# Dilated attention with scores in 64x32 fp32 tiles, values per four blocks, and a bias table spread by class late in the program

## The chip, the cores and the metric

The kernel runs on one core of a Trainium2 chip, as one launch. The metric is the device time of a run in microseconds (us). The core has a matrix engine (PE, with its weight loads shown apart as PEld), a vector engine (DVE), a scalar engine (ACT), a general engine (POOL), and a queue (SP) from which this kernel issues nearly all of its DMA transfers. Each engine works through its own list of instructions in order and waits by semaphores for the others.

## The reference

One transformer block in fp32: 1024 tokens, width 1024, eight attention heads and eight gated DeltaNet heads of 64 side by side, then a gated feed-forward part. The attention is dilated in three branches that are merged by their log-sum-exp, which is one softmax over keys of different multiplicity:

```
DILATED_BRANCHES = ((128, 1), (512, 4), (2048, 16))
...
    steps = qi + band - kj
    in_window = (steps >= 0) & (steps <= band)
    bias = rel_bias.astype(jnp.float32)[_t5_bucket(jnp.maximum(steps, 0) * dilation)]
    s = jnp.einsum('bhrnqd,bhrnkd->bhrnqk', qb * dh ** -0.5, kw) + bias[None, :, None, None]
...
    w = jax.nn.softmax(jnp.stack(lses), axis=0)
    o = jnp.sum(w[..., None] * jnp.stack(outs), axis=0)
```

A query sees every key at a distance of up to 128, and further back only keys at a distance that is a multiple of 4 (up to 512) or of 16. Keys farther than one block of 128 thus count only if they have the query's position modulo 4, its class. The DeltaNet half takes projections q, k, v through a causal convolution of width 4 and SiLU, solves a unit triangular system in each chunk of 64, and scans over 16 chunks.

## The kernel before

The program has stages one behind another. From the start to about 100 us it normalizes and projects. delta(0) and then delta(1) treat four DeltaNet heads each: preparation, convolution of v (`delta_v`), a triangular inverse (`delta_inverse`), and a scan over chunks (`delta_scan`). Then `attend` does the attention, for four pairs of heads (hp) and eight query blocks of 128 (qb), 32 units in all; the output projection follows, and from about 720 us the feed-forward part, which the change leaves alone.

PE is kept at work by fill. `fill[0]` is a generator of projection matmuls: in delta(1) these are the gate projection `g_z`, the attention projections `g_a` (queries and keys) and `g_va` (values), and later the output projection `wo`. `turn(name)` asks the table FILL how many us of fill go ahead of a step, `ahead` takes them, and in `attend` a budget FRONT is spread over the first units. With these settings the library that builds the program sets the final order of each engine's list.

In delta(1) three chains meet. The first is v: a load `xp_v` per pair of heads (`fetch`, `_.pj`), the convolution taps on ACT and DVE (tile `vd`, lines L550 and L552), SiLU on ACT (L556), transposes on PE (`trv`, L874), and a scaling on DVE (`vb`, L877). It runs for two pairs. The second is the inverse on DVE: tile `nt` is loaded from `lt_d` (L852), scaled (L887), and 31 steps of two instructions follow (`tm` L898, `tt` L902). The third leads from the inverse to the scan: `tt` is written out as `tn_d`, read back as `tn` (L905, L907), turned on DVE (`U`, L935), and used by PE for `lv` (L930).

The attention of a unit (hp, qb): scores `S` of a head against all keys up to the query's block. They are made in fp32r (a faster fp32 mode of PE) with K split in a high and a low part (`KS`, `KL`) and Q in a tile `QS` of 128 rows that carries both parts of Q, so that two matmuls of up to 512 columns make one stretch of scores (L1327, L1328). `att_load` makes these tiles for every head on ACT, DVE and POOL. DVE adds the bias and takes the running minimum of the negated scores (L1331), ACT takes the exponential (L1336), POOL scales by the reciprocal of the sum (L1338). One unit later (AT=1) PE transposes the result block by block (`tr`, L1351), which ACT and DVE copy to `et`; three units later (AV=3), for two units at a time, PE multiplies by the values (`y`, L1372), a head in each half of the columns of the array.

The bias is a table `R_d` of 1152 numbers for each head (negative scores, with a huge number where a key is not seen). When the values of the first pairs are stored (`va`, L1102), eight broadcast transfers spread a row of it over 128 rows as `Rb_d` (L1121, 576 KB each); in the profile they are issued at 69 to 79 us. `att_load` reads a skewed view of it as `ng` (512 KB for a head).

## Time and profile before

| what | value |
|---|---|
| runs | 1385.23, 1391.03, 1392.99 us, median 1391.03 |
| profiled execution | 1385.31 us, its span 1383.3 us |
| PE, DVE, ACT, POOL busy | 1336.5, 875.4, 659.7, 268.4 us |
| chain that ended last | PE 71%, DVE 14%, DMA 5%, ACT 4% |
| attention with its fill on PE | 451.6 to 654 us |

A number is one execution's. Busy time of PE is nearly the whole span, but a busy PE is not a PE at its peak: matmuls are pipelined, and an instruction's duration holds its latency. What one costs is seen from the distance of one start to the next. Where an engine idles, the row of the instruction behind the gap shows in square brackets how long it waited and for whom.

### The profile page before, as it was taken

Reading aid. Unit: us, or ns where it says so; the run is one execution under the profiler, and the core shown is the slowest. Engines: PE = TensorE matmul, PEld = TensorE weight load, DVE = VectorE, ACT = ScalarE, POOL = GpSimd, SP = SyncE. Lnnn points to the kernel's source line nnn. Section 1 sums busy time; section 2 is a strip of 40 time slices with the busy share of each in tenths; the row PEclk is TensorE's granted clock in tenths of the full one; section 3 lists DMA queues with packets and bytes.
Section 4 is the critical chain, followed back from the end, with each engine's and each line's share of the span. In section 5 each row is a group of like instructions: output and inputs, shape, how many; then the busy total and the mean of one; then the engine's idle time right before and its main releaser. Section 6 shows DMA issues by size and latency. Waiting matters only on the chain.

```text
span 1383.3 us, 24383 instructions
## 1 busy us (share of the span) xinstructions
PE 1336.5 (97%) x8984; PEld 1105.9 (80%) x8984; DVE 875.4 (63%) x1678; ACT 659.7 (48%) x1285; POOL 268.4 (19%) x250
## 2 busy tenths in 40 slices
PE   8998999999999999999999999999999999999998
PEld 5777887888889877687877788888888888888876
DVE  3688583657847242766248978666675776474497
ACT  4497514347233454775168633333333333454455
POOL 2345303324213434542261000000000000000000
PEclk9999899999999999999999999999999999999999
DMA  8665574475362546531675346445453665765585
GB/s 313 228 191 171 163 212 159 138 221 164 120 175 82 170 139 178 150 100 66 211 242 168 113 154 209 142 160 175 151 177 123 218 215 183 251 226 193 191 272 192
DMA packets 169871, 245.64 MB, mean 178 GB/s; under 512 B 32566, under 2 KB 73831, under 8 KB 169752
## 3 DMA queue, kind: packets, MB, share of 16 engines
q1 hardware_dynamic: 169752, 244.08, 54.7%
q8 instruction: 71, 1.16, 0.3%
q14 instruction: 48, 0.39, 0.1%
HBM read 181.27 MB, written 67.48 MB: 180 GB/s over the span
## 4 chain that ended last, share of the span: by engine, by line
PE 71%; DVE 14%; DMA 5%; ACT 4%; issue 3%; POOL 2%; SPq 0%; POOLq 0%; DVEq 0%; ACTq 0%
PE wua L1621 9%; PE wga L1621 8%; PE X L1821 6%; PE wgc L1621 4%; PE wuc L1621 4%; PE g_a L589 4%; PE wo L589 3%; PE Z L1821 3%; PE Y L1821 2%; PE wub L1621 2%; PE wgb L1621 2%; PE y L1372 2%; PE g_va L615 2%; DVE tm L898 2%; PE f L250 2%
## 5 line engine op out<-in xcount | busy, mean ns | idle before, releaser
L1611 DVE TENSOR_TENSOR wl_db<-wr_db,wh_db 128x512 fp32r<-128x512 f32 x77 | 53.0, 691 | 67.2 <-ACT wh_db L1610 67.0
L1610 ACT CAST wh_db<-wr_db 128x512 fp32r<-128x512 f32 x77 | 47.4, 620 | 86.3 <-PE X L1821 37.8
L1331 DVE CUSTOM_DVE_ANT_0 X<-S,ng 128x512 f32<-128x512 f32 (+3 forms) x64 | 36.6, 587 | 60.9 <-PE S L1328 53.7
L1338 POOL TENSOR_SCALAR X<-X,sc 128x128 f32<-128x128 f32 (+7 forms) x64 | 48.6, 762 | 90.5 <-DVE sc L1337 77.5
L1821 PE MATMUL X<-wl_db,wh_da 128*128 128x512 f32 x160 | 62.4, 390 | 0.3 <-DVE wl_db L1611 0.3
L1821 PE MATMUL X<-wh_db,wl_da 128*128 128x512 f32 x160 | 62.3, 389 | 0.0
L1821 PE MATMUL X<-wh_db,wh_da 128*128 128x512 f32 x160 | 62.2, 389 | 0.0
L1336 ACT ACTIVATE X<-X,sc 128x128 f32<-128x128 f32 (+7 forms) x64 | 49.4, 773 | 26.7 <-DVE sc L1331 25.1
L1611 DVE TENSOR_TENSOR wl_da<-wr_da,wh_da 128x512 fp32r<-128x512 f32 x77 | 52.9, 687 | 3.5 <-ACT wh_da L1610 3.5
L1610 ACT CAST wh_da<-wr_da 128x512 fp32r<-128x512 f32 x77 | 47.4, 616 | 14.0 <-DMA wr_da<-ao_d 7.1
L589 PE MATMUL wo<-yh,wh_wo 128*128 128x512 f32 x128 | 52.0, 406 | 0.0
L589 PE MATMUL g_a<-hh,wh_a 128*128 128x512 f32 x128 | 51.4, 402 | 0.0
L589 PE MATMUL wo<-yh,wl_wo 128*128 128x512 f32 x128 | 51.1, 399 | 0.0
L589 PE MATMUL wo<-yl,wh_wo 128*128 128x512 f32 x128 | 50.6, 395 | 0.5 <-DVE yl L1439 0.5
L589 PE MATMUL g_a<-hl,wh_a 128*128 128x512 f32 x128 | 50.6, 396 | 0.0
L589 PE MATMUL g_a<-hh,wl_a 128*128 128x512 f32 x128 | 50.4, 394 | 0.0
L1351 PE MATMUL tr<-ident,X 128*128 128x128 f32 x288 | 44.1, 277 | 4.3 <-ACT et L1356 1.6
L1610 ACT CAST wh_wg_s<-wg_s 128x512 fp32r<-128x512 f32 x33 | 20.6, 623 | 56.1 <-PE wuc L1621 23.8
L1351 PEld LDWEIGHTS tr<-ident,X 128*128 128x128 f32 x288 | 32.6, 140 | 15.3 <-POOL X L1338 6.8
L1610 ACT CAST wh_wg<-wr_wg 128x512 fp32r<-128x512 f32 x31 | 19.3, 621 | 46.2 <-PE wua L1621 18.9
L1610 ACT CAST wh_wu_s<-wu_s 128x512 fp32r<-128x512 f32 x33 | 20.4, 621 | 43.6 <-PE wga L1621 17.2
L230 POOL TENSOR_TENSOR wl_wo<-wr_wo,wh_wo 128x512 fp32r<-128x512 f32 x24 | 31.8, 1326 | 48.5 <-ACT wh_wo L229 44.3
(554 smaller groups left out, 4341.9 us busy)
## 6 DMA issues: line engine op xcount, KB each, us to landing
wm<-in_wada SPq DMA_DIRECT2D x44, 512.0 KB, 6.4
wr_da<-ao_d SPq DMA_DIRECT2D x77, 256.0 KB, 2.9
wr_wu<-in_wu SPq DMA_DIRECT2D x50, 256.0 KB, 2.8
wr_wg<-in_wg SPq DMA_DIRECT2D x48, 256.0 KB, 2.9
ao_d<-a SPq DMA_DIRECT2D x44, 256.0 KB, 2.5
wr_wd<-in_wdn SPq DMA_DIRECT2D x44, 256.0 KB, 3.0
wr_db<-wt_d SPq DMA_DIRECT2D x44, 256.0 KB, 2.7
ao_d<-as SPq DMA_DIRECT2D x33, 256.0 KB, 2.0
```

The lines of the kernel that those rows point to most:

```text
L230: (eng or nc.gpsimd).tensor_tensor(out=lo[:, :n], in0=raw[:, :n], in1=hi[:, :n].bitcast(F32), op=ALU.subtract)
L250: nc.tensor.matmul(first[bank], a[:, w0], b[k][:, cs], start=(k == 0 and n_ == 0), stop=(k == KT - 1 and n_ == 2))
L589: last[0] = nc.tensor.matmul(ps, a[:, w0], b[k0 + k4][:, cs], start=(i == 0), stop=(i == n - 1))
L615: last[0] = nc.tensor.matmul(ps[:, :n], a[k][:, ts_], b[:, w0], start=(i == 0), stop=(i == 23))
L1331: nc.vector.tensor_tensor_reduce(out=X[:, c0:c1], in0=ps[:, 0 : c1 - c0], in1=ng[:, u + c0 : u + c1], scale=1.0, scalar=(3e38 if m is None ...
L1336: nc.scalar.activation(X[:, 0:nk], X[:, 0:nk], AF.Exp, scale=-1.0, bias=m, accum_out=sc[:, 2:3])
L1338: nc.gpsimd.tensor_scalar(out=X[:, 0:nk], in0=X[:, 0:nk], scalar1=sc[:, 3:4], scalar2=0.0, op0=ALU.mult, op1=ALU.add)
L1351: nc.tensor.transpose(ps[:, (kb - c0) * P : (kb - c0 + 1) * P], X[:, kb * P : kb * P + P], ident)
L1610: nc.scalar.copy(hi, src)
L1611: (eng or nc.vector).tensor_tensor(out=lo, in0=src, in1=hi.bitcast(F32), op=ALU.subtract)
L1621: nc.tensor.matmul(ps, a[:, w0], b, start=(first and k == 0 and n_ == 0), stop=(k == 3 and n_ == 2), skip_group_check=True,)
L1821: nc.tensor.matmul(bank[b], a[:, ts_], w, start=(first and n_ == 0), stop=(last and n_ == 2), skip_group_check=True,)
```

## The change

It rewrites the attention and the way of its bias table.

- Table: it holds 1120 numbers sorted by class (448, 448, 224) in place of 1152. It is first copied into `R4_d` (four rows a head, one for each class, four transfers of 8x2x256 and one of 32x1x224), then spread to `Rb_d` by eight transfers of 4x32x736 (377 KB each, in rows of 2944 bytes). They are issued behind the stores of the first values (`table`, called in `va_end`), in delta(1).
- Storing: `spill` writes queries and keys sorted by class in each block (position 4j+r goes to 32r+j), with the factor -0.125 on queries, on ACT. The values are stored sorted likewise.
- Loading: q and k come once for a pair of heads, without the split tiles: four casts and products on ACT, DVE and POOL for each head are gone. The bias tile `bt` (480 columns a head) takes four loads a pair, the values one load and eight small ones (`vf`, the far keys' values).
- Scores: plain fp32, in tiles of 64 rows by 32 columns of the array: two heads (row halves) times four classes (column quarters). A block has eight matmuls against its 256 near keys and, from block 2 on, eight against the 32n far keys of its own class, chained by `issue_after`. A head's row of scores is at most 480 wide and one DVE instruction treats it.
- Transposes: 1, 2, 3, 3, 3, 3, 4, 4 for a head's blocks 0 to 7 (184 in all, 288 before), two units behind the scores (AT=2).
- Values: once for four blocks, 120 matmuls of 64x128, 64 of 64x2x32 and 32 of 64x4x32 (288 of 64x128 before).
- Fill: entries of FILL for the old steps go, and BACK spreads the output projection evenly over the units behind the first 14, 12 matmuls a unit.

Cut to its core:

```diff
-XB, ETB, AT, AV = 5, 6, 1, 3
+XB, ETB, AT, AV = 8, 4, 2, 3
+BACK = 16 * 4 * 0.64
...
+        for h in {3: (0, 1), 4: (2, 3), 5: (4, 5), 6: (6,), 7: (7,)}.get(tb, ()):
+            nc.sync.dma_start(
+                bass.AP(
+                    tensor=Rb_d.tensor, offset=Rb_d[h, 0:1, :].offset + 96,
+                    ap=[[32 * 768 - 32, 4], [768, 32], [1, 736]],
+                ),
+                bass.AP(tensor=R4_d.tensor, offset=R4_d[h, 0:1, :].offset, ap=[[736, 4], [0, 32], [1, 736]]),
+            )
...
-                nc.sync.dma_start(Rb_d[tb], R_d[tb : tb + 1, :].to_broadcast([P, 1152]))
+                with tc.issue_after(stored[0].ins):
+                    table(tb)
...
-                nc.tensor.matmul(ps[:, 0 : c1 - c0], QS[:, qs], KS[:, c0:c1], start=True, stop=False)
-                nc.tensor.matmul(ps[:, 0 : c1 - c0], QS[:, qs], KL[:, c0:c1], start=False, stop=True)
+            for near in range(0 if f else 1, 2):
+                for r in range(4):
+                    for e in (1, 0):
+                        rows, qs = slice(64 * e, 64 * e + 64), slice(32 * r, 32 * r + 32)
+                        if near:
+                            out, src = pss[e][qs, f:w], k[rows, b0 * P : n * P + P]
+                        else:
+                            out = pss[e][qs, 0:f].rearrange("p (m j) -> p m j", j=32)
+                            src = by_class(k[rows])[:, 0:n, r]
+                        with tc.issue_after(mm.ins) if mm else ExitStack():
+                            mm = nc.tensor.matmul(out, by_class(q[rows])[:, n, r], src, start=True, stop=True)
...
+            if i >= first:
+                ahead(BACK / (len(units) + AV - first))
...
-            if i >= AV and units[i - AV][1] % 2:
+            if i >= AV and units[i - AV][1] % 4 == 3:
```

Instructions also change places outside the attention. The first place is DVE in delta(1), around the convolution of v for the second pair (`vd_4040` before, `vd_4046` now) and the inverse, which begins with `nt`. DVE before:

```order
L552 SCALAR_TENSOR_TENSOR vd_4040<-xp_v_4041,cw,vd_4040 128x1023
L552 SCALAR_TENSOR_TENSOR vd_4040<-xp_v_4041,cw,vd_4040 128x1022
L552 SCALAR_TENSOR_TENSOR vd_4040<-xp_v_4041,cw,vd_4040 128x1021
L887 TENSOR_TENSOR nt_3827<-nt_3827,bpr_3829 128x1024
L877 TENSOR_TENSOR vb_4048<-trv_0_4049,beta 128x512
L877 TENSOR_TENSOR vb_4048<-trv_1_4192,beta 128x512
L898 TENSOR_TENSOR tm_0_4202<-nt_3827,tt_4199 128x31
L902 TENSOR_TENSOR tt_4199<-tt_4199,tm_0_4202 128x31
L898 TENSOR_TENSOR tm_1_4205<-nt_3827,tt_4199 128x60
```

The taps of the second pair stood ahead of the inverse. DVE now, first at the head of the inverse:

```order
L862 TENSOR_TENSOR vb_3842<-trv_0_3843,beta 128x512
L862 TENSOR_TENSOR vb_3842<-trv_1_4040,beta 128x512
L872 TENSOR_TENSOR nt_3830<-nt_3830,bpr_3832 128x1024
L883 TENSOR_TENSOR tm_0_4208<-nt_3830,tt_4205 128x31
L887 TENSOR_TENSOR tt_4205<-tt_4205,tm_0_4208 128x31
```

The products of the first pair are followed by `nt` at once. And DVE now at the end of the inverse, 58 rows on:

```order
L883 TENSOR_TENSOR tm_30_4298<-nt_3830,tt_4205 128x31
L887 TENSOR_TENSOR tt_4205<-tt_4205,tm_30_4298 128x31
L537 SCALAR_TENSOR_TENSOR vd_4046<-xp_v_4047,cw,vd_4046 128x1023
L537 SCALAR_TENSOR_TENSOR vd_4046<-xp_v_4047,cw,vd_4046 128x1022
L537 SCALAR_TENSOR_TENSOR vd_4046<-xp_v_4047,cw,vd_4046 128x1021
L862 TENSOR_TENSOR vb_4054<-trv_0_4055,beta 128x512
L862 TENSOR_TENSOR vb_4054<-trv_1_4198,beta 128x512
L920 STREAM_TRANSPOSE U_0_4635<-tn_4302 32x8x32 x4
```

The three taps and the two products `vb` have moved behind the last step of the inverse, next to `U`.

The same pair's transposes `trv` on PE, which read `vd`, before (row 1500 of PE's list, 229 rows ahead of the first `lv`):

```order
L615 MATMUL g_z_4_4301<-wl_z_0_4056,hh_93 128x256
L615 MATMUL g_z_4_4301<-wh_z_0_4055,hh_94 128x256
L874 MATMUL trv_0_4049<-ident,vd_4040 128x128 x4
L874 MATMUL trv_1_4192<-ident,vd_4040 128x128 x4
L615 MATMUL g_z_4_4301<-wh_z_0_4055,hl_102 128x256
L615 MATMUL g_z_4_4301<-wl_z_0_4056,hh_94 128x256
```

And now (row 1549, 183 rows ahead of `lv`; the rows between are 48 `g_z`, 96 `g_a` and 39 `g_va`):

```order
L600 MATMUL g_z_5_4335<-wh_z_3_4079,hl_108 128x256
L600 MATMUL g_z_5_4335<-wl_z_3_4080,hh_100 128x256
L859 MATMUL trv_0_4055<-ident,vd_4046 128x128 x4
L859 MATMUL trv_1_4198<-ident,vd_4046 128x128 x4
L600 MATMUL g_z_6_4363<-wh_z_0_4061,hh_93 128x256
L600 MATMUL g_z_6_4363<-wh_z_0_4061,hl_101 128x256
```

They moved down by two groups of `g_z`, and still stand ahead of all the rest of the fill.

The second place is SP's queue, before, where both loads `xp_v` go out early (rows 189 and 192 of its list; `nt` is row 211):

```order
L1210 DMA xp_v_3832<-pj_d 128x1024
L1220 DMA cv_d<-cv_3405 128x1024
L1102 DMA va_d<-va_4_3919 128x2x128
L1210 DMA xp_v_4041<-pj_d 128x1024
L1220 DMA cv_d<-cv_3430 128x1024
```

And now, around `nt` (row 211) and the second `xp_v` (row 221):

```order
L1103 DMA Rb_d<-R_d 4x32x736
L837 DMA nt_3830<-lt_d 128x1024
L1160 DMA wm_4_5080<-in_wada 128x2x512
L1160 DMA wm_6_5082<-in_wada 128x2x512
L1103 DMA Rb_d<-R_d 4x32x736
L1117 DMA va_d<-va_4_3923 32x4x256
L1103 DMA Rb_d<-R_d 4x32x736 x2
L1117 DMA va_d<-va_5_3953 32x4x256
L1103 DMA Rb_d<-R_d 4x32x736 x2
L1117 DMA va_d<-va_6_3983 32x4x256
L1103 DMA Rb_d<-R_d 4x32x736
L1238 DMA xp_v_4047<-pj_d 128x1024
```

One table transfer goes out ahead of `nt`, and seven ahead of the second `xp_v`.

The third place is PE in a late unit of the attention (pair 3, block 6 before, blocks 5 and 3 now). Before, wide matmuls of one head alternate with transposes and fill:

```order
L1327 MATMUL S_6_512_7640<-KS_6968,QS_6967 128x384
L1328 MATMUL S_6_512_7640<-KL_6969,QS_6967 128x384
L1327 MATMUL S_6_0_7649<-KS_6978,QS_6977 128x512
L1328 MATMUL S_6_0_7649<-KL_6979,QS_6977 128x512
L1351 MATMUL tr_5_0_7661<-ident,X_5_7582 128x128 x2
L1327 MATMUL S_6_512_7653<-KS_6978,QS_6977 128x384
L1328 MATMUL S_6_512_7653<-KL_6979,QS_6977 128x384
L1351 MATMUL tr_5_0_7661<-ident,X_5_7582 128x128 x2
L1351 MATMUL tr_5_4_7667<-ident,X_5_7582 128x128 x2
L589 MATMUL wo_1_1_7566<-yh_6713,wh_wo_1_7344 128x512
```

Now the last near scores of one block are followed by the transposes of the block two units back:

```order
L1356 MATMUL S_5_7741<-raw_3_7075,raw_3_7074 32x256
L1356 MATMUL S_5_7740<-raw_3_7075,raw_3_7074 32x256
L1356 MATMUL S_5_7741<-raw_3_7075,raw_3_7074 32x256
L1356 MATMUL S_5_7740<-raw_3_7075,raw_3_7074 32x256
L1356 MATMUL S_5_7741<-raw_3_7075,raw_3_7074 32x256
L1356 MATMUL S_5_7740<-raw_3_7075,raw_3_7074 32x256
L1387 MATMUL tr_3_7771<-ident,X_3_7646 128x128 x3
L1387 MATMUL tr_3_7770<-ident,X_3_7640 128x128 x3
L1356 MATMUL S_6_7783<-raw_3_7075,raw_3_7074 32x192
```

Small matmuls of the two heads take turns, and each unit visits the scores and the transposes once.

More of the change, by code (lines that the diff above doesn't have):

```diff
@@ L179, in build @@
     nc.sync.dma_start(rb[0:32, :], I["rel"])
-    for t, cs in zip(tbl, (slice(0, T), slice(T, T + P))):
+    for t, cs in zip(tbl, (slice(0, 896), slice(896, 1120))):
         nc.sync.dma_start(t, I["tbl"][:, cs])
@@ L1311, in build, with far @@
     loaded = {}
     ybanks = {}
[L1314 to L1330 removed]
+    def far(n):
+        return 32 * n if n > 1 else 0
@@ new lines, in att_score, with att_turn @@
+            X.append(x)
+        return X, mm
+    turned = {}
+    def att_turn(hp, n, X, mm):
+        f = far(n)
+        if n % 4 == 0:
+            for h in (2 * hp, 2 * hp + 1):
+                turned[h] = pa.tile([P, 4, 4, P], F32, name=f"et{h}_{n // 4}", tag="et", bufs=ETB)
+        s0, s1 = (1, 2) if n == 0 else (0, 2 + (n > 1) + (n > 5))
+        cols = {0: f, 1: f + (P if n else 0), 2: 0, 3: P}
+        pss = [tbank(f"tr{2 * hp + e}_{n}") for e in range(2)]
+        with turn(f"et{hp}_{n}"):
+            for e in (1, 0):
+                for i in range(s0, s1):
+                    with tc.issue_after(mm.ins) if mm else ExitStack():
+                        mm = nc.tensor.transpose(
+                            pss[e][:, i * P : i * P + P], X[e][:, cols[i] : cols[i] + P], ident
+                        )
+        for e in (1, 0):
+            (nc.vector.tensor_copy if e else nc.scalar.copy)(
+                turned[2 * hp + e][:, n % 4, s0:s1].rearrange("p b q -> p (b q)"), pss[e][:, s0 * P : s1 * P]
+            )
+        return turned[2 * hp], turned[2 * hp + 1]
@@ L1390, in attend @@
         xs, ets = {}, {}
+        first = EARLY * TB + 3 + AV
         for i in range(len(units) + AV):
@@ L1952, in _bucket_table @@
 def _bucket_table():
-    d = 1023 - np.arange(1152)
+    i = np.arange(64)
+    near = [128 * (1 - q) + 4 * (31 - i) + 3 - t for q in range(2) for t in range(7)]
+    d = np.concatenate([*near, 4 * (255 - np.arange(224))])
     dist_f = np.maximum(d, 1).astype(np.float32)
```

271 lines of the change are left out of this document (132 added, 139 removed).

## The prediction

> **What bounds the kernel now.** I read the page first, then windows over the two stages that the change touches, then the timelines of PE and DVE there, and the chain that ended last.
>
> ```profile
> PE 1336.5 (97%) x8984; PEld 1105.9 (80%) x8984; DVE 875.4 (63%) x1678; ACT 659.7 (48%) x1285; POOL 268.4 (19%) x250
> ...
> GB/s 313 228 191 171 163 212 159 138 221 164 120 175 82 170 139 178 150 100 66 211 242 168 113 154 209 142 160 175 151 177 123 218 215 183 251 226 193 191 272 192
> ...
> PE 71%; DVE 14%; DMA 5%; ACT 4%; issue 3%; POOL 2%; SPq 0%; POOLq 0%; DVEq 0%; ACTq 0%
> ...
> L1331 DVE CUSTOM_DVE_ANT_0 X<-S,ng 128x512 f32<-128x512 f32 (+3 forms) x64 | 36.6, 587 | 60.9 <-PE S L1328 53.7
> ...
> L1336 ACT ACTIVATE X<-X,sc 128x128 f32<-128x128 f32 (+7 forms) x64 | 49.4, 773 | 26.7 <-DVE sc L1331 25.1
> ```
>
> PE is busy nearly all the time and holds 71% of the last chain. So what PE no longer has to do in the attention is time won, and what makes PE stop in delta(1) is time lost. Two windows show both stages (columns: busy time of PE, PEld, DVE, ACT, POOL, then the granted clock, DMA share, GB/s):
>
> ```profile
> 355.00:386.00 31.00, 31.00 (x175) 27.23 (x175) 21.93 (x45) 8.30 (x18) 11.08 (x8) 1.00 0.42 120
> ...
> 451.60:654.00 202.40, 194.65 (x1436) 158.21 (x1436) 100.86 (x316) 119.94 (x267) 85.86 (x88) 1.00 0.45 135
> ```
>
> In the attention DVE and ACT have half of their time free. In the last 31 us of delta(1)'s inverse PE does not rest at all.
>
> **The attention on PE, before.** The fill inside that window is 350 matmuls of 512 columns and 30 of 256 (the same window for these two lines alone):
>
> ```profile
> 451.60:654.00 202.40, 93.69 (x350) 62.95 (x350) 1.00 0.45 135
> ```
> ```profile
> 451.60:654.00 202.40, 3.81 (x30) 3.66 (x30) 1.00 0.45 135
> ```
>
> What one costs is the distance of starts:
>
> ```profile
> 365.67 0.39 PE L589 MATMUL g_a<-hh,wl_a 128*128 128x512 f32 x1
> ...
> 366.35 0.39 PE L589 MATMUL g_a<-hh,wl_a 128*128 128x512 f32 x1
> ```
> ```profile
> 385.97 0.28 PE L615 MATMUL g_va<-wh_va,hl 128*128 128x256 f32 x1
> 386.09 0.28 PE L615 MATMUL g_va<-wl_va,hh 128*128 128x256 f32 x1
> 386.30 1.20 PE L930 MATMUL lv<-tn,dt 32*32 32x32 f32 x64
> ```
> ```profile
> 639.86 0.40 PE L1327 MATMUL S<-KS,QS 128*128 128x512 f32 x1
> 640.10 0.39 PE L1328 MATMUL S<-KL,QS 128*128 128x512 f32 x1
> 640.32 0.40 PE L589 MATMUL wo<-yh,wh_wo 128*128 128x512 f32 x1
> ```
> ```profile
> 647.21 1.06 PE L1351 MATMUL tr<-ident,X 128*128 128x128 f32 x8
> 648.03 0.48 PE L589 MATMUL wo<-yh,wl_wo 128*128 128x512 f32 x1
> ...
> 650.83 3.50 PE L1372 MATMUL y<-et,va 128*64 128x128 f32 x60
> 654.26 0.50 PE L589 MATMUL wo<-yh,wl_wo 128*128 128x512 f32 x1
> 654.60 0.39 PE L589 MATMUL wo<-yh,wh_wo 128*128 128x512 f32 x1
> ```
>
> Fill: three starts in 0.68 us are 0.227 us each, and 0.12 for 256 columns, so 350 x 0.227 + 30 x 0.12 = 83.1 us. The attention itself takes 202.4 - 83.1 = 119.3. Of it, scores: 0.23 us per 512 columns; the loops give 73,728 columns, 33.1 us. Transposes: eight in 0.82, 288 x 0.1025 = 29.5. Values: 60 records in 3.43, 0.057 each; a plain fp32 matmul leaves two records, so 576 x 0.057 = 32.8. These make 95.4; the other 23.9 are changes of shape and waits.
>
> **Part one: the attention after.** Transposes 184 x 0.1025 = 18.9. Values: 304 records of 128 columns and 128 of 64, 304 x 0.057 + 128 x 0.029 = 21.0. Scores have no like in the trace, since no tile of 64 rows by 32 columns runs before. Each direction alone does:
>
> ```profile
> 19.78 0.66 PE L307 MATMUL sums<-sq,onesr 128*32 128x256 f32 x8
> 20.23 1.04 PE L311 MATMUL sums<-xt,wbg 128*32 128x256 f32 x14
> ```
> ```profile
> 319.82 1.05 PE L798 MATMUL kk_q<-qd,kd 64*128 64x128 f32 x14
> 320.71 0.31 PE L798 MATMUL kk_k<-kd 64*128 64x128 f32 x1
> ```
>
> By the transposes a column of a lone fp32 pass takes 0.8 ns. Column quarters: eight passes of 256 columns in 0.45 us, 56 ns for 205, nearly four at once. Row halves: 14 passes of 128 columns in 0.89, 64 ns for 102, with the first one's start-up in it, nearly two at once. The new scores of a pair of heads are 16 passes over 1920 near and 864 far columns, 178,000 columns in all four pairs: 143 us alone, 18 if eight run at once, 40 if only the quarters do. I take 18, since both directions are seen and nothing in the rows speaks against their product; 40 is the bound. The work is then 18 + 18.9 + 21.0 = 58.
>
> Of the 23.9 beside the work I keep 18. The step out of one shape costs 0.34 - 0.23 = 0.11 us (654.26 to 654.60); 32 visits to the scores and 8 to the values, in and out, make 9, transposes some 3, and 6 stay for waits. For waits it speaks that DVE's and ACT's widths fall from 4608 to 2784 columns a head (36.6 and 49.4 us to about 22 and 30), that two units lie between scores and transposes, and that 12 fill matmuls (2.7 us) stand in each late unit. So 76 instead of 119.3: **43 won**. Bounds: 48 with 13 beside the work, 21 with scores at 40. Taking away the casts on ACT, DVE and POOL costs and wins nothing of its own, as these engines wait for PE. Early in the program eight table transfers of 576 KB vanish; I put that at nothing, since DMA has 5% of the last chain in all.
>
> **Part two: delta(1).** The edit puts the table's transfers into SP's queue, and with them the second `xp_v` went back, and the taps of `vd` on DVE behind the whole inverse. PE's `trv`, which needs them, kept its place ahead of 183 fill rows. PE works in order. So it must stand still until the inverse is done. The rows of this chain:
>
> ```profile
> 342.22 3.92 DVE L552 SCALAR_TENSOR_TENSOR vd<-xp_v,cw,vd 128x1023 f32<-128x1023 f32 x3 [0.39 <-ACT vd L550]
> 346.06 1.22 DVE L887 TENSOR_TENSOR nt<-nt,bpr 128x1024 f32<-128x1024 f32 x1
> ...
> 349.25 0.18 DVE L898 TENSOR_TENSOR tm<-nt,tt 128x31 f32<-128x31 f32 x1
> ```
> ```profile
> 378.25 0.19 DVE L902 TENSOR_TENSOR tt<-tt,tm 128x31 f32<-128x31 f32 x1
> 386.27 1.78 DVE L935 STREAM_TRANSPOSE U<-tn 32x256 f32<-32x256 f32 x4 [7.83 <-DMA tn<-tn_d]
> ```
> ```profile
> 346.24 1.07 ACT vd L556
> 347.35 0.67 PE trv L874 x4
> ...
> 378.47 2.92 DMA tn_d<-tt
> 381.40 4.78 DMA tn<-tn_d
> ```
> ```profile
> 342.21 0.34 SPq L852 DMA_DIRECT2D nt<-lt_d  x1
> ```
>
> From the first tap (342.22) to `trv` (347.35) are 5.1 us. The inverse is 1.2 for `nt` and 349.25 to 378.44 for the steps, 30.4 in all. `nt` was there by 346.06. So now: inverse 346.1 to 376.5, `trv` at 381.6, eight transposes 0.9, then the rows up to `lv`: 48 + 39 of 256 columns and 96 of 512, 87 x 0.12 + 96 x 0.227 = 32.2. `lv` starts at 414.7, where it was 386.3: 28.4 later. Nothing hides it: before, the last `g_va` (386.09) ran straight into `lv`, and the fill that PE could do meanwhile stands behind `trv`. On ACT the SiLU waits with two gate activations behind it, on DVE only `vb` and `U`, all within the stop. The round trip of `tn` (7.7 us, 378.47 to 386.18) leaves the path, and `U` is turned ahead: 0.5 won.
>
> Two costs come on top. First, PE's clock after a rest:
>
> ```profile
> 131.30:134.10 2.80, 0.00 (x0) 0.00 (x0) 2.80 (x5) 0.08 (x1) 0.95 (x1) 1.00 0.24 81
> 135.10:145.20 10.10, 10.10 (x76) 10.10 (x76) 7.04 (x12) 10.10 (x33) 2.99 (x2) 0.50 0.65 173
> ```
>
> A rest of some 2.8 us was followed by 10.1 us at 0.50 of the clock, 5 us lost. A rest of over 20 us should do no less: +5, with 0 and 5 as bounds. The Trainium skill ("TensorE: Matmul & The Clock Gate", Part 1) says that about 3.4 us without work halve the clock and about 3.4 us of steady work bring it back; by that the loss would be 1.7 and the sum 3 us lower. The trace shows three times as long a spell.
>
> Second, one table transfer now goes ahead of `nt`: 0 to 3 us, I take 1.5. **Lost: 28.4 + 5 + 1.5 - 0.5 = 34.4.**
>
> **Sum.** Against the profiled execution of 1385.3: 1385.3 - 43 + 34.4 = 1377. The median of the runs is 0.4% above that execution, about as much as a measurement of this kernel can tell from no change (0.5%, 7 us).
>
> **The rivals.**
>
> Row halves take turns: scores at 40, won only 21, 1385.3 - 21 + 34.4 = 1399. It decides from scores of 27 us on (43 - 34.4 = 9 more than 18). For it: no such tile is in the trace. Against: both directions run at once by themselves. Waits in the attention of 20 us more would end there too, but the free time of DVE and ACT speaks against that.
>
> The second `xp_v` comes late, behind seven table transfers:
>
> ```profile
> Rb_d<-R_d SPq DMA_DIRECT2D x8, 576.0 KB, 7.0
> ```
>
> Spread over all DMA engines, 3.0 MB at the 313 GB/s of the page's best slice are 10 us, and `xp_v` lands long before 376. One after another at 7 us each they take 49: `xp_v` at 392, `trv` at 398, 17 more, 1394. Between lies a mechanism with its own price: their outermost dimension is 4, and if only four of the engines carry them, 3.0 MB take four times 9.6, 39 us from 342.5, so `xp_v` at 381, `trv` at 387 or 388 after ACT's first product, 6 more, 1383. The Trainium skill ("DMA: Bandwidth & Descriptors", on why a DMA increments its semaphore by 16, how many engines) has just this: the number is the largest up to 16 that divides the slowest dimension of both sides. No row of before can tell, since its transfers have 128 rows outermost.
>
> The stop does not come, or DVE is done sooner than I read: then only the attention counts, 1342 to 1350. The order of the rows speaks against it.
>
> **How the numbers follow.** The forecast, 1367 to 1386 with its own bounds: 0.50. Row halves in turn, or waits (1390 to 1402): 0.17. The late `xp_v` (1381 to 1395): 0.22. No stop (1342 to 1350): 0.05. A stop as read with more won, 1360 to 1367: 0.06. Faster by over 7 us (below 1378): 0.35 of the forecast's half and the last two, 0.46; slower (above 1392): most of the first rival and some of the second, 0.23; between: 0.31. The range that leaves out no more than 2 in 10 is 1358 to 1401.
>
> **What would show it.** Right: PE idle from about 356 to 381 with the gap put down to `vd` on ACT, a granted clock of 0.5 behind it, `lv` near 418 to 421, scores at some 0.43 us for eight near matmuls, the attention's own share near 76 us. Wrong: no gap ahead of `trv`; scores at twice that; or `xp_v` landing after the inverse.

## The result, and the profile after

The changed kernel takes 1380.03 us (median of 8 runs, 1375.27 to 1382.03), the kernel before 1389.02 us beside it: a ratio of 0.9931, with a 95% interval of 0.9909 to 0.9953, so it is faster by some 0.7%. The prediction was 1377. The profiled execution of the changed kernel took 1375.27 us, the fastest of its eight, 10.0 less than that of before. Inside these 10 us lie two large terms, as forecast: the attention gives 36, the stop in delta(1) takes 28.

The page of the changed kernel (busy time of the engines, PE's busy tenths in 40 slices of 34 us, PE's granted clock in tenths):

```profile
PE 1315.4 (96%) x9440; PEld 1075.4 (78%) x9440; DVE 834.7 (61%) x1604; ACT 618.3 (45%) x1237; POOL 246.2 (18%) x250
...
PE   8998999997599999999999999999999999999998
...
PEclk9999899999799999999999999999999999999999
```

PE is busy 21 us less, and slice 11 (343 to 378 us) is new: PE is busy 5 tenths of it, and its clock falls. Windows over that place show it closer (busy time of PE, PEld, DVE, ACT, POOL, then clock, DMA share, GB/s). Before, PE was busy all 31 us from 355 to 386.

```profile
341.00:355.00 14.00, 5.71 (x29) 5.50 (x28) 7.78 (x21) 0.40 (x2) 0.00 (x0) 0.62 0.59 190
355.00:386.00 31.00, 22.22 (x139) 21.40 (x140) 21.10 (x49) 4.67 (x9) 0.95 (x1) 0.82 0.41 146
```

PE's rows with a wait in brackets, the changed kernel, in delta(1):

```profile
339.74 1.97 PE L859 MATMUL trv<-ident,vd 128*128 128x128 f32 x8 [4.92 <-ACT vd L541]
354.72 0.58 PE L600 MATMUL g_z<-wh_z,hh 128*128 128x256 f32 x1 [8.29 <-ACT zt L621]
362.42 0.39 PE L600 MATMUL g_z<-wh_z,hh 128*128 128x256 f32 x1 [2.50 <-ACT zt L621]
370.15 0.58 PE L600 MATMUL g_z<-wh_z,hh 128*128 128x256 f32 x1 [3.11 <-ACT zt L621]
376.06 0.39 PE L600 MATMUL g_z<-wh_z,hh 128*128 128x256 f32 x1 [1.48 <-ACT zt L621]
380.90 1.10 PE L859 MATMUL trv<-ident,vd 128*128 128x128 f32 x8 [1.70 <-ACT vd L541]
```

The stop is there, but in pieces. PE did not come to `trv` and wait once; it waited four times in `g_z` ahead of it, for the gate activation `zt` on ACT, and only 1.70 us in front of `trv`. ACT itself waited for transfers (ACT, then SP's queue, then the share of busy DMA engines in 40 slices from 340 to 385 us):

```profile
354.28 0.38 ACT L621 ACTIVATE zt<-g_z 128x256 f32<-128x256 f32 x1 [13.27 <-DMA va_d<-va]
...
374.59 1.15 ACT L535 ACTIVATE vd<-xp_v,cw 128x1024 f32<-128x1024 f32 x1 [4.49 <-DMA xp_v<-pj_d]
```
```profile
338.86 0.63 SPq L1103 DMA_DIRECT2D Rb_d<-R_d  x1
339.73 0.34 SPq L837 DMA_DIRECT2D nt<-lt_d  x1
...
359.15 4.21 SPq L1238 DMA_DIRECT2D xp_v<-pj_d  x1
```
```profile
DMA  4969995222522222252226942555258243220640
```

The 2's are the table: a share of two tenths is what 4 of 16 engines make while the other 12 stand idle. The stores of the values behind it in the queue (`va_d`, 14.3 us from issue to landing) keep ACT's buffers. The second `xp_v` left at 359.15 and let ACT begin at 374.59. DVE, in the same order of time:

```profile
347.80 1.23 DVE L872 TENSOR_TENSOR nt<-nt,bpr 128x1024 f32<-128x1024 f32 x1 [5.37 <-DMA va_d<-va]
...
372.27 0.19 DVE L887 TENSOR_TENSOR tt<-tt,tm 128x31 f32<-128x31 f32 x1
375.77 3.92 DVE L537 SCALAR_TENSOR_TENSOR vd<-xp_v,cw,vd 128x1023 f32<-128x1023 f32 x3 [3.31 <-ACT vd L535]
```

In the attention, the window that answers to 451.60:654.00 of before, all lines and then the fill alone; and one stretch of units with blocks 2 to 4:

```profile
484.90:679.20 194.30, 191.61 (x2002) 140.51 (x2002) 75.97 (x255) 83.73 (x226) 66.05 (x89) 1.00 0.53 157
```
```profile
484.90:679.20 194.30, 125.29 (x489) 88.08 (x489) 1.00 0.53 157
```
```profile
605.82 0.78 PE L1356 MATMUL S<-raw,raw 64*32 64x64 f32 x32
606.52 0.44 PE L1387 MATMUL tr<-ident,X 128*128 128x128 f32 x2
609.65 0.83 PE L1356 MATMUL S<-raw,raw 64*32 64x96 f32 x32
610.40 0.66 PE L1387 MATMUL tr<-ident,X 128*128 128x128 f32 x4
...
613.43 0.39 PE L574 MATMUL wo<-yh,wl_wo 128*128 128x512 f32 x1
613.75 0.88 PE L1356 MATMUL S<-raw,raw 64*32 64x128 f32 x32
614.56 0.88 PE L1387 MATMUL tr<-ident,X 128*128 128x128 f32 x6
615.19 0.48 PE L574 MATMUL wo<-yh,wh_wo 128*128 128x512 f32 x1
```

A unit's scores (8 near matmuls and 8 far ones, each of two passes and so two records) take 0.70, 0.75 and 0.81 us up to the transposes: 32 far columns more for each of 16 passes cost 0.055 us. At 0.8 ns a column one after another they would cost 0.41: seven to eight run at once.

### The profile page after: what moved, and what is told of

Same layout as the page of the kernel before. It is cut to its first block, busy times and chain, and to the rows that moved or that the text cites. A ratio compares the mean times of both kernels' runs of the same rounds, so it can differ in the third digit from the quotient of the medians.

```text
span 1373.6 us, 25071 instructions
## 1 busy us (share of the span) xinstructions
PE 1315.4 (96%) x9440; PEld 1075.4 (78%) x9440; DVE 834.7 (61%) x1604; ACT 618.3 (45%) x1237; POOL 246.2 (18%) x250
## 4 chain that ended last, share of the span: by engine, by line
PE 44%; DVE 4%; DMA 1%; issue 1%; ACT 1%; POOLq 0%; POOL 0%; DVEq 0%; ACTq 0%
PE wua L1671 9%; PE wga L1671 9%; PE X L1871 6%; PE wgc L1671 4%; PE wuc L1671 4%; PE Z L1871 3%; PE wgb L1671 2%; PE Y L1871 2%; PE wub L1671 2%; PE wo L574 2%; DVE wl_db L1661 1%; DVE x L1584 1%; DMA wr_db<-wt_d 0%; DVE wl_da L1661 0%; DVE y L1944 0%
## 5 line engine op out<-in xcount | busy, mean ns | idle before, releaser
L1361 DVE CUSTOM_DVE_ANT_0 X<-S,bt 128x128 f32<-128x128 f32 (+7 forms) x64 | 30.8, 517 | 72.2 <-PE S L1356 71.9
L600 PE MATMUL g_z<-wh_z,hh 128*128 128x256 f32 x128 | 40.6, 318 | 17.6 <-ACT zt L621 16.7
L1365 ACT ACTIVATE X<-X,sc 128x128 f32<-128x128 f32 (+7 forms) x64 | 37.0, 580 | 39.7 <-DVE sc L1361 39.7
L1367 POOL TENSOR_SCALAR X<-X,sc 128x128 f32<-128x128 f32 (+7 forms) x64 | 36.5, 575 | 89.7 <-DVE sc L1366 89.5
L574 PE MATMUL g_a<-hh,wl_a 128*128 128x512 f32 x128 | 50.1, 391 | 0.0
L600 PEld LDWEIGHTS g_z<-wh_z,hh 128*128 128x128 f32 x128 | 27.9, 218 | 19.2 <-ACT zt L621 17.7
L600 PE MATMUL g_z<-wh_z,hl 128*128 128x256 f32 x128 | 39.2, 306 | 0.0
```

What stands on the lines that cost most here:

```text
L574: last[0] = nc.tensor.matmul(ps, a[:, w0], b[k0 + k4][:, cs], start=(i == 0), stop=(i == n - 1))
L600: last[0] = nc.tensor.matmul(ps[:, :n], a[k][:, ts_], b[:, w0], start=(i == 0), stop=(i == 23))
L1361: nc.vector.tensor_tensor_reduce(out=x[:, 0:w], in0=pss[e][:, 0:w], in1=bt[:, e, 480 - w : 480], scale=1.0, scalar=3e38, op0=ALU.add, op1= ...
L1365: nc.scalar.activation(x[:, 0:w], x[:, 0:w], AF.Exp, scale=-1.0, bias=sc[:, 0:1], accum_out=sc[:, 2:3])
L1367: nc.gpsimd.tensor_scalar(out=x[:, 0:w], in0=x[:, 0:w], scalar1=sc[:, 3:4], scalar2=0.0, op0=ALU.mult, op1=ALU.add)
```

## The experiments

In all of them the stop is read as the time from the start of delta(1)'s first `trv` to that of its first `lv` on PE: 46.5 us before, 74.4 in the changed kernel, so 27.9 of stop. The stages ahead of that `trv` vary by some 8 us between executions of equal lists, so times of day are not compared. The times beside which each run is set are of the kernel before on the same chip: 1387.0 for runs 1 to 4, 1386.1 for 5 to 8, 1389.2 for 9 and 10, 1386.4 for 11.

The two columns on the right are of each run's profiled execution.

| run | time, us (median) | ratio to before (95%) | `trv` to `lv` | `lv` to last `wo` |
|---|---|---|---|---|
| before | 1389.0 | 1 | 46.5 | 352.7 |
| changed | 1380.0 | 0.9931 (0.9909, 0.9953) | 74.4 | 314.8 |
| 1 | 1376.5 | 0.9924 (0.9900, 0.9948) | 69.3 | 315.2 |
| 2 | 1360.1 | 0.9812 (0.9785, 0.9840) | 46.6 | 316.9 |
| 3 | 1403.2 | 1.0112 (1.0085, 1.0138) | 52.8 | 358.1 |
| 4 | 1400.3 | 1.0092 (1.0067, 1.0116) | 58.6 | 350.9 |
| 5 | 1361.1 | 0.9813 (0.9782, 0.9843) | 46.7 | 324.7 |
| 6 | 1400.7 | 1.0105 (1.0077, 1.0134) | 46.6 | 366.9 |
| 7 | 1359.9 | 0.9803 (0.9776, 0.9830) | 46.5 | 325.6 |
| 8 | 1357.9 | 0.9791 (0.9767, 0.9815) | 50.2 | 323.7 |
| 9 | 1364.8 | 0.9831 (0.9810, 0.9853) | 52.0 | 317.8 |
| 10 | 1372.8 | 0.9902 (0.9874, 0.9931) | 48.4 | 315.9 |
| 11 | 1356.3 | 0.9765 (0.9737, 0.9793) | 46.4 | 328.7 |

**Run 1: the lists of the changed kernel, transfers on all engines.**

```diff
-ap=[[32 * 768 - 32, 4], [768, 32], [1, 736]],
+ap=[[768, 32], [32 * 768 - 32, 4], [1, 736]],
...
-ap=[[736, 4], [0, 32], [1, 736]]
+ap=[[0, 32], [736, 4], [1, 736]]
```

> The changed kernel with the eight table transfers written with 32 rows outermost in place of 4 (the same bytes), so that they can use all DMA engines. Each engine's list of instructions stays as in the changed kernel: the taps of vd behind the inverse, trv 183 fill rows ahead of lv. Theory (the place of the taps makes PE stop, the slow transfers add little): xp_v and nt land some us earlier, PE stands in one piece in front of trv until the inverse has ended, the first lv starts at 408 to 415 us where the changed kernel had 414.1, and the time is 1372 to 1381 us. Rival (the transfers on four engines make the stop, the place of the taps doesn't matter): no gap over 3 us in front of trv, lv at 386 to 392, 1350 to 1358 us.

The theory holds: 1376.5 us, and of 27.9 us of stop 22.9 stay. (Beside its kernel before, the time alone does not tell this run from the changed kernel: the intervals of 0.9924 and 0.9931 overlap.) The share of busy DMA engines (40 slices from 335 to 392 us), then PE, then ACT with the second `xp_v`, then DVE's taps:

```profile
DMA  4431147847998989999988000000009003549713
```
```profile
359.35 0.58 PE L600 MATMUL g_z<-wh_z,hh 128*128 128x256 f32 x1 [5.83 <-ACT zt L621]
381.78 1.97 PE L859 MATMUL trv<-ident,vd 128*128 128x128 f32 x8 [9.44 <-ACT vd L541]
```
```profile
366.03 1.15 ACT L535 ACTIVATE vd<-xp_v,cw 128x1024 f32<-128x1024 f32 x1 [1.85 <-DMA xp_v<-pj_d]
380.67 1.06 ACT L541 ACTIVATE vd<-vd 128x1024 f32<-128x1024 f32 x1 [13.22 <-DVE vd L537]
```
```profile
376.66 3.92 DVE L537 SCALAR_TENSOR_TENSOR vd<-xp_v,cw,vd 128x1023 f32<-128x1023 f32 x3
```

Now all engines carry the table (8's and 9's), and ACT begins 18.4 us after the first `trv` (347.61) in place of 34.9. Then it waits 13.22 us for taps that stand behind the inverse and begin with the end of its last step. Most of the wait moved from `g_z` to `trv`, and stayed. `lv` came at 417.0, 2 us outside the expected range, as this execution was 8 us late at its first `trv` already.

**Run 2: as run 1, transfers as early as in the kernel before.**

```diff
-                with tc.issue_after(stored[0].ins):
-                    table(tb)
+                table(tb)
```

> As the run before, and the table transfers are issued as early in the program as in the kernel before (without the order behind the stores of the values). The second xp_v, the taps and trv then stand where they stood in the kernel before. Theory: PE does not stop, lv starts at 386 to 389, the attention keeps its 36 to 38 us, and the time is 1389 - 37 = 1352 us, between 1348 and 1357. Rival (part of the attention's gain was only work that the stop in delta(1) had delayed or spread, or the early transfers cost something before delta(1)): 1360 or more.

The stop is gone (46.6 us), but the time is 1360, not 1352. That is the lower end of the rival, and it is the rival's second half that came: the early transfers cost something before delta(1). Two waits of PE stand in delta(0):

```profile
157.15 1.97 PE L859 MATMUL trv<-ident,vd 128*128 128x128 f32 x8 [4.99 <-ACT vd L541]
...
173.85 0.79 PE L574 MATMUL g_qd<-hh,wh_qd 128*128 128x512 f32 x1 [5.18 <-ACT sp_kd L1133]
```

With the transfers early, the first pair's taps stand 24 rows further down DVE's list, behind the products `qk` and `dt`. The two waits are 10.2 us together, and in the ten us behind each the clock is at 0.76. The first `trv` of delta(1) comes at 349.4, where the changed kernel had 339.7.

**Run 3: the transfers in their form of the changed kernel, moved behind the second `xp_v`.**

```diff
...
-for h in {3: (0, 1), 4: (2, 3), 5: (4, 5), 6: (6,), 7: (7,)}.get(tb, ()):
+for h in {0: (0, 1), 1: (2, 3), 2: (4, 5), 3: (6, 7)}.get(tb, ()) if c else ():
...
```

> The changed kernel with the eight table transfers, as they are (4 rows outermost), moved behind the second xp_v, two at each of the first four calls of va_end for the second four heads. The taps now stand after the eighth step of the inverse in place of behind the last one. Theory: PE stops for as long as the taps are late, some 5 to 12 us, lv starts at 392 to 400, and the time is 1356 to 1365 us. Rival (a list of the same transfers on four engines anywhere in delta(1) holds up stores and loads enough to stop PE): lv at 405 or later, 1370 us or more.

The stop was as the theory had it (6.3 us, `lv` at 396.3), the time was not: 1403, which lies in the rival's range, though the stop that the rival meant did not come. Both missed where the transfers went. They wait in SP's queue behind stores of the second values, and the last leaves when the attention wants its bias (SP's queue, then PE):

```profile
505.40 0.60 SPq L1103 DMA_DIRECT2D Rb_d<-R_d  x1
506.10 4.44 SPq L1302 DMA_DIRECT2D bt<-Rb_d  x4
```
```profile
514.46 1.11 PE L1355 MATMUL S<-raw,raw 64*32 64x256 f32 x16 [11.76 <-DVE sc L1360]
```

From `lv` to the last `wo` 43 us are lost. This wait is one part of it. Another lies in the scan, where SP's queue stands 26.4 us in front of a weight load `wr_a` (it waits for POOL to free the buffer), with loads `zl` of the scan behind it. On the page the clock is at 6 tenths in the slices from 455 to 525 us.

**Run 4: the kernel before, its own table transfers ordered as in the changed kernel.**

```diff
...
-                nc.sync.dma_start(Rb_d[tb], R_d[tb : tb + 1, :].to_broadcast([P, 1152]))
+                with tc.issue_after(stored[0].ins):
+                    nc.sync.dma_start(Rb_d[tb], R_d[tb : tb + 1, :].to_broadcast([P, 1152]))
```

> The kernel before, its attention untouched, with its own eight table transfers (576 KB, 128 rows outermost) ordered behind the stores of the first values as in the changed kernel. The taps now stand after the sixteenth step of the inverse, trv 166 rows ahead of lv (229 before), and five transfers go ahead of the second xp_v. Theory (the order alone makes the stop): trv at about 367 where PE comes to it at about 355, 10 us and half clock behind it, lv at 396 to 404, and the time is 1397 to 1407 us, 10 to 18 over the kernel before. Rival (only transfers on few engines make the stop): 1385 to 1392 us.

The time is the theory's: 1400.3 us, 13 over before, `lv` at 404.4. The attention is untouched and the transfers have 128 rows outermost, so their place by itself makes a stop of 12 us. But the stop is not where the theory had it (PE, then ACT):

```profile
358.02 0.58 PE L615 MATMUL g_z<-wh_z,hh 128*128 128x256 f32 x1 [5.67 <-ACT zt L636]
```
```profile
357.59 0.38 ACT L636 ACTIVATE zt<-g_z 128x256 f32<-128x256 f32 x1 [10.60 <-DMA va_d<-va]
```

PE waits ahead of `trv`, for ACT, and ACT waits for stores `va_d` that the transfers hold up, though here all engines carry them. The second `trv` (373.55) follows the fill without a wait. So the taps in the middle of the inverse did not stop PE in this run; the stores behind the transfers did, and the clock was at half behind the wait.

**Run 5: small copies early, the transfers behind the load `tn`, all engines.**

```diff
-                with tc.issue_after(stored[0].ins):
-                    table(tb)
+                table(tb)
...
+    with tc.issue_after(marks["tn"].ins):
+        spread()
```

> The changed kernel with the small copies of the table early, and the eight transfers to Rb_d (32 rows outermost, all engines) behind the load tn of delta(1). All lists then read in delta(0) and delta(1) as in the kernel before; the transfers are issued from about 388 us on, ahead of the attention's bias loads. Theory (both stops came from the lists, and nothing else in delta costs time): from the first trv of delta(1) to lv 46 to 47 us as before, no stop in delta(0) either, the attention's 36 us all kept, 1387 - 36 = 1351 us, between 1347 and 1355. Rival (the transfers hold up the loads zl and bt at the start of the attention): PE stops there, 1357 us or more.

No stop in delta(0) or delta(1) (46.7 us), yet 1361 again: the rival. The end of the scan (PE, then SP's queue):

```profile
459.05 0.66 PE L1062 MATMUL yt<-ident,o 128*128 128x128 f32 x2 [6.28 <-DVE o L1052]
```
```profile
452.34 3.35 SPq L213 DMA_DIRECT2D wr_a<-in_wd  x3
455.80 0.37 SPq L1042 DMA_DIRECT2D zl<-zg_d  x1
```

The last loads `zl` stand behind three weight loads, PE waits 6.28 us, and its clock is at 0.59 in the window from 460 to 470 us. `lv` to `wo` is 9.9 us longer than in the changed kernel.

**Run 6: as run 5, 4 rows outermost.** Its edit is run 1's, undone.

> As the run before, with the transfers to Rb_d in their form of the changed kernel (4 rows outermost). In delta the lists are the same. Theory (four engines carry them, some 9.6 us each one behind the other, and what is issued behind them waits): eight take until about 467 us or later, the loads zl wait some us each and the bias loads bt come late, PE stops at the end of the scan and in front of the first bias, 8 to 20 us more than the run before, 1359 to 1371 us. Rival (off the chain, the form of a transfer costs nothing): within 3 us of the run before.

1400.7, 39.7 us over run 5: the direction is the theory's, the size twice what it gave, and the rival is out. (By the prediction's sum eight transfers on four engines take 39 us, 4.8 each and not 9.6.) PE's two longest waits, then SP's queue:

```profile
463.38 0.69 PE L1062 MATMUL yt<-ident,o 128*128 128x128 f32 x2 [6.52 <-DVE o L1052]
...
505.54 0.80 PE L574 MATMUL g_a<-hh,wh_a 128*128 128x512 f32 x1 [15.68 <-ACT va L1116]
```
```profile
456.64 2.77 SPq L213 DMA_DIRECT2D wr_a<-in_wd  x3
```

Not only loads wait behind the transfers; the stores of `va` do too, ACT's buffers stay full, and PE's fill stands still. The speed of the transfers is not all of it, though. The expectation that the lists are the same holds up to the load `tn`, but not in the scan: in run 5 the last transfer leaves at 434, here six of the eight leave from 460 on. And ahead of the weight load at 456.64, with a load `zl` behind it, SP's queue stood 32.2 us and waited for POOL to free the buffer, with 5 GB/s or less under way from 431 to 456 us. On the page the clock is at 5 and 7 tenths in the slices from 456 to 526 us. How the 40 us are shared between the slow transfers and the other list is not shown.

**Run 7: as run 5, three fill matmuls between scores and transposes.**

```diff
-BACK = 16 * 4 * 0.64
+BACK = 16 * 3 * 0.64
...
+for hp in range(2, 4):
+    for n in range(8):
+        FILL.setdefault(f"et{hp}_{n}", 0.64)
```

> As the run with the order as before (all engines), and in 14 units of the attention's last two pairs three of the twelve fill matmuls stand between the scores and the transposes, the other nine behind them, the same fill in all. It adds one change of shape a unit. Theory (a change costs about 0.1 us whatever stands behind it, so that the shape changes beside the work don't shrink with the work): 14 x 0.1 to 0.2 = 1.4 to 2.8 us more in this stretch, the time up by as much at most. Rival (the fill there covers waits for the exponential, which the transposes stood behind): the stretch 1 us or more shorter.

The last two pairs take 90.3 us with 177 fill matmuls, 84.9 with 170 in run 5; less 0.227 each, 50.1 against 46.3. Of the 3.8 us, 2.7 are waits (3.7 against 1.0; one of 2.96 is new), and the clock was at half behind it (PE, then the window, with a clock of 0.96 where run 5 has 1.00):

```profile
648.38 1.07 PE L1361 MATMUL S<-raw,raw 64*32 64x224 f32 x32 [2.96 <-DVE sc L1366]
```
```profile
571.70:662.00 90.30, 86.59 (x1015) 64.56 (x1014) 41.01 (x137) 35.27 (x99) 28.98 (x42) 0.96 0.52 153
```

Four hundredths of 90.3 us are 3.6, so the waits and the clock are more than the whole difference. The same stretch has 46.3 to 49.6 us in the other runs with this attention, and the times are the same (1359.9 and 1361.1). The rival's gain isn't there, and a price of a change of shape can't be read from this run: the theory is neither shown nor out.

**Run 8: as run 5, the low parts of the weights taken off POOL.**

```diff
+            if name[0] == "a" or name[:2] == "va":
+                nc.scalar.copy(lo[:, :n], raw[:, :n])
+            else:
...
```

> As the run with the order as before (all engines); the low parts wl_a and wl_va are copied on ACT in place of POOL's subtraction (a copy of the raw weights, so the subtraction is left out). It tests why the inverse took 29.2 us before and 23.3 in the changed kernel. Theory (a DVE step with two tensor inputs waits for a POOL subtraction that runs beside it, 1.40 us in place of 0.42): no step of the inverse over 0.5 us, the inverse 23 to 24 us, where the run with POOL's subtractions has 28 to 30. As PE's fill ends about when tn comes, the time changes by less than 4 us. Rival (the steps are long for another reason, such as their place in the inverse or PE running beside them): 28 to 30 us in both.

The kernel of this run leaves out the subtraction for `wl_a` and `wl_va`, which hold a copy of the raw weights. The theory holds. The inverse takes 23.3 us in place of 29.2, and the time changes by 3, less than the intervals can tell. (`trv` to `lv` is 50.2 us all the same, since the clock was at half for some us around the first `trv`.) Steps of the same size, run 5 with its POOL row, then run 8:

```profile
356.69 1.40 DVE L887 TENSOR_TENSOR tt<-tt,tm 128x247 f32<-128x247 f32 x1
```
```profile
356.42 4.25 POOL L215 TENSOR_TENSOR wl_a<-wr_a,wh_a 128x512 fp32r<-128x512 f32 x3 [8.13 <-PE g_z L600]
```
```profile
361.66 0.42 DVE L890 TENSOR_TENSOR tt<-tt,tm 128x247 f32<-128x247 f32 x1
```

**Runs 9, 10 and 11: other places for the transfers, all engines.** Run 9 puts them right behind the second `xp_v`, run 10 behind the load `tn` of delta(0), run 11 gives each pair's two transfers a place behind the bias loads of the pair ahead (the edit of run 11, cut):

```diff
+        if hp < 3:
+            with tc.issue_after(marks["bt"].ins):
+                spread(hp + 1)
         return bt
```

> As the run with the order as before (all engines), but the eight transfers to Rb_d stand in SP's queue right behind the second xp_v and ahead of nt of delta(1), in one bunch. The lists of delta(0), of delta(1)'s taps and of the scan's loads zl then all read as in the kernel before or in the run with early transfers. Theory (the 10 us that the run with the order as before lost at the end of the scan were the last zl, queued behind other loads): no gap at the last yt, from lv to the last wo 315 to 317 us in place of 324.7; eight transfers ahead of nt can make the inverse late by up to 5 us; the time is 1349 to 1356 us. Rival (the loss at the attention's start is not from the place of zl): 1359 us or more.

> As the run before, with the eight transfers (all engines) in delta(0)'s scan, behind its load tn, about 205 to 260 us into the program. Nothing then stands ahead of nt or xp_v of delta(1). Theory: as the run before without the delay of nt, if delta(0)'s loads zl aren't held up: 1348 to 1354 us. Rival (the transfers hold up zl in delta(0)'s scan as they did in delta(1)'s): a gap of 3 to 6 us at a yt of delta(0), 1354 to 1362 us.

> As the run with the order as before (all engines), but only the first pair's two transfers to Rb_d stand behind the load tn; those of each later pair follow the bias loads of the pair ahead of it, inside the attention. SP's queue at the end of the scan then reads as in the run with early transfers: each zl next to the store of yt, no weight load between. Theory (the table cost 5 to 12 us wherever its 3 MB stood as one bunch in SP's queue in delta, and a quarter of it costs next to nothing there): delta(0) and the taps as before, no gap at the last yt, from lv to the last wo 315 to 318 us, 1347 to 1355 us, the fastest of all. Rival (inside the attention, the transfers delay the next pair's loads, and PE stops in front of a new pair's scores): lv to the last wo over 322 us, 1358 us or more.

Run 9 agrees with what run 5 left open: with `zl` in place, `lv` to `wo` is 317.8 us, 0.8 above the theory's range. But the time, 1364.8, is in the rival's range, since the 8 transfers now hold up the loads `qd` ahead of the first `trv` and ACT's stores behind it (52.0 us of `trv` to `lv`). Run 10 holds up `zl` in delta(0), as its rival said, and was slower still than that gave (PE's rows of run 9, then of run 10):

```profile
339.35 2.05 PE L783 MATMUL kk_q<-qd,kd 64*128 64x128 f32 x15 [8.60 <-DMA qd<-cv_d]
```
```profile
310.76 0.66 PE L1062 MATMUL yt<-ident,o 128*128 128x128 f32 x2 [4.93 <-DVE o L1052]
```

Run 11, with 0.75 MB at a place in place of 3 MB, is the fastest by its median: 1356.3 us, 30 under before, 1 above the expected range. Its interval overlaps those of runs 2, 5, 7 and 8, so it is not shown to be faster than run 2 or 5. Its 328.7 from `lv` to `wo` are of the slowest of its six executions (1363.8 us), the profiled one, so they say little about the other five. About 7 of them are a spell at half clock, told at the end. Some 5 more lie in the attention (200.0 us from its first scores to its last values, 194.9 in run 2). No wait over 0.5 us stands in front of a new pair's scores, so the rival's stop is not there; where the 5 us come from stays open.

## Why the prediction was right, and where its terms were off

**The sum.** 1385.3 - 43 + 34.4 gave 1377. In the profiled executions it was 1385.3 - 36 + 28 and 2 us less elsewhere, 1375.3. Both large terms were read too large by 6 or 7 us, and the two errors cancelled. That the sum came within 3 us of the median is luck in part: the steps were not that good.

**The attention, 36 in place of 43.** The window has 194.3 us, the fill in it 489 x 0.227 = 111.0, so the attention is 83.3 where it was 119.3. The work came as worked out: scores with all eight tiles at once (18), six transposes in 0.63 us (614.56 to 615.19), 0.105 each, so 19.3 for 184 (18.9 was taken); with values at 21 that makes 58. The step that failed is "of the 23.9 beside the work I keep 18": 83.3 - 58 leaves 25, as much as before. Waits are only 2.7 of it (194.30 less 191.61 of busy time), where 6 were kept; so the changes of shape have some 22 in place of 12. Added up from the distances of the starts in this window, 8 of the 22 lie between a unit's last scores and what follows, 5 at the ends of the fill, 5 at the first fill matmul behind a change, 3 around the values, and 1 is fill a little slower than 0.227. A visit to the scores alone costs 0.3 us beside its passes (0.81 less 768 columns x 0.8 ns = 0.61, and 0.32 - 0.23 on entry, 613.43 to 613.75), 32 of them 9 us, which had been taken for scores and values together. Before, waits had 7.7 of the 23.9 (202.40 less 194.65), so the changes had some 16: they cost more now, though there are fewer of them (136 in the rows of the window, 199 before). That the part beside the work stayed the same is the sum of two opposite moves.

**The stop, 27.8 in place of 34.4** (`lv` at 414.1, 386.3 before). Term by term (the 0.5 us won by turning `U` ahead lies behind `lv`):

- `nt` behind one transfer: 347.80 against 346.06, 1.7 late; 1.5 was taken.
- The inverse, with `nt`: 347.80 to 372.46, 24.7 us in place of the 30.4 taken from before. This is the step that was most wrong, 5.7. While PE stood still, no weights were split on POOL (0.00 us in the first window), and no step was long; run 8 shows that POOL's subtractions make the steps long.
- Behind the inverse, the taps did not begin at once: 3.31 us for ACT's product, for which `xp_v` was late. The rival had this mechanism, with `xp_v` at 381 and 6 us; ACT's product began at 374.59.
- From the first tap to `trv` 5.1, as taken; from `trv` to `lv` 33.2, 33.1 as taken.
- Half clock: 5 were taken behind the stop, 0 came there. The pieces of work between the pieces of the stop ran at 0.62 and 0.82 of the clock, where PE had to wait anyway, and behind the last wait it was full. The spell was read too long, too: behind the wait of 8.29 us the `g_z` matmuls start 0.21 us apart until 359.4 and 0.12 from then on, so 4.7 us at half clock, where 10.1 had been taken from before. In run 1, with one wait of 9.44 us ahead of `trv`, the spell behind it cost 2 (35.2 from `trv` to `lv`).

28.4 + 1.7 - 5.7 + 3.3 gives 27.7. So PE stood until the inverse was done, and 3.3 us longer; but that the inverse held it is shown for run 1 only. Three chains are late at once, all through the place of the transfers:

- The taps behind the inverse. In run 1 ACT's product was there at 367.18 (366.03 + 1.15), and the taps began with the end of the inverse at 376.66: there their place in the list held `trv` for 9.5 us. In the changed kernel it held nothing at the end. The inverse ended at 372.46, ACT's product at 375.74 (374.59 + 1.15), and the taps at 375.77 could not have begun sooner in any list.
- The late `xp_v`, which set `trv` in the changed kernel, by these 3.3 us.
- The stores `va_d`, which held ACT and through it `g_z`. "PE idle with the gap put down to `vd`" was wrong in place: 15.4 of the 17.1 us of gaps from 341 on stand in front of `g_z`. In run 4 these stores make the stop without the taps.

Runs 2 and 5, which take the transfers away from this place, have no stop in delta(1). Run 1, which only makes them faster, keeps 22.9 us of it. So the place of the transfers makes the stop; what each chain would cost by itself is not shown. Of the other signs that the prediction named, the scores came (the rounds of near matmuls start 0.216 us apart, 0.43 for the two rounds); the half clock behind `trv`, `lv` at 418 to 421 and an attention near 76 us did not.

**The rivals.** Row halves in turn: out, by the 0.055 us above. The late `xp_v`: the mechanism is there, its condition was the four engines, and its link was the last one. Without it the second `trv` comes 7 us sooner behind the first (34.2 in place of 41.2, run 1), of which half clock behind it takes back 2, so the stop is 5 us shorter. The Trainium skill ("DMA: Bandwidth & Descriptors", on why a DMA increments its semaphore by 16) makes the number of engines the largest up to 16 that divides the slowest dimension of both sides; the trace agrees, with a DMA share of 2 tenths at 4 rows outermost and 9 tenths at 32. No stop: out.

**What the prediction put at nothing.** "Early in the program eight table transfers vanish; I put that at nothing" holds, but the other side of it was not seen: the table's transfers, issued as one bunch, cost something at every place that runs 1 to 10 gave them. By the sum the change would be worth 36 us without its stop (an estimate), and the best run got 30 of them.

## What to carry to other kernels

A transfer that nobody waits for is not free: look at what stands behind it in its queue (loads, and stores that free an engine's buffers), and at what a scheduler moves because of it; divide it, and give each part a place near its use. Write the outermost dimension of both sides of a transfer so that all engines share it, since here the same bytes with 4 rows outermost made a stop longer by 5 us at one place, and at another the program slower by 40, there with another order in the queue too. Before a wait is put down to the one cause that was looked for, see which of the late chains ended last. When small matmuls replace large ones, count the changes of shape as a term of its own: here it rose from some 16 to some 22 us while the work between the changes fell from 95 to 58.

## What the runs showed of the hardware that was not expected

A DVE step with two tensor inputs next to a POOL subtraction takes 1.40 us in place of 0.42. Each of the six long steps of run 5 ends 0.25 to 0.28 us after a POOL subtraction does, whatever its own size. The inverse has 29.2 us with six of them beside it, in each of seven executions (before and runs 2, 5, 6, 7, 9 and 11), and 23.3 without (the changed kernel, runs 1 and 8). The Trainium skill ("SBUF — State Buffer", section "SBUF: two separate sides") describes a pair of ports shared by DVE and GpSimd (POOL here) that one instruction holds as a lock until it ends, against DVE steps with two SBUF inputs too; the rows agree with a lock and not with a share.

The clock can fall without a long rest. In run 11's profiled execution (windows as above):

```profile
380.00:390.00 10.00, 8.89 (x147) 8.02 (x148) 2.80 (x7) 3.80 (x10) 2.48 (x2) 1.00 0.96 226
390.00:400.00 10.00, 10.00 (x139) 8.54 (x133) 3.08 (x7) 3.04 (x8) 1.25 (x2) 0.51 0.69 247
400.00:410.00 10.00, 10.00 (x191) 8.92 (x184) 3.65 (x8) 2.41 (x7) 0.96 (x1) 0.64 0.01 2
```

No gap there is over 0.8 us; PE had run `lv` in 32x32 tiles and waits between them, as in run 5, where the clock stayed at 1.00. Clocks of 0.51 and 0.64 over ten us each are some 17 us at half clock. From the first `lv` to the last `yt` this execution took 71.7 us, run 2 64.8: these 7 us are about the distance of this execution from its median. What sets the spell off in one execution and not in another stays open.
